# The seams between five parts of a layer stack, reordered by token tile, and the last expert step in half tiles

## The chip, the cores and the metric

The kernel runs on one core of a Trainium2 chip. TensorE (PE) multiplies, VectorE (DVE) and ScalarE (ACT) do elementwise work and read PSUM, GpSimd (POOL) does small things here (the powers of the norms, memsets, a few DMA issues), and SyncE (SP) issues most DMAs. Each engine works through its own instructions in order and waits on semaphores for the others. The metric is device time in microseconds of one launch.

## The reference, cut to what matters

Three blocks run one after the other on 256 tokens of width 1024, all in float32. The first ends in a 16-expert feed-forward layer and a norm. The second is two dense half layers around a token mixing (projections, a convolution, a chunked matrix memory, an output projection). The third is a stack of attention and recurrent layers, and its first step is a norm and a projection of the same 256 tokens.

```python
def rmsnorm(x, g):
    xf = x.astype(jnp.float32)
    y = xf * lax.rsqrt(jnp.mean(xf * xf, axis=-1, keepdims=True) + EPS)
    return (y * g.astype(jnp.float32)).astype(x.dtype)
...
    xl_new = xl_new + gt2 * expert_choice_ffn(modulate(xl_new, g_ffn, sh2, sc2), w_router, w1, w3, w2)
...
    return rmsnorm(xl, g_final)
...
def half_ffn(h, shift, scale, gate, g_pre, g_post, w13, w2):
    u = modulate_2(rmsnorm_2(h, g_pre), shift, scale)
    return h + 0.5 * gate * rmsnorm_2(swiglu(u, w13, w2), g_post)
...
        h_lat = half_ffn(h_lat, ml[:, 0], ml[:, 1], ml[:, 2], g[0], g[1], w13_a[l], w2_a[l])
        h_lat, h_ctx_new = token_mixing(
            h_lat, h_ctx, (ml[:, 3], ml[:, 4], ml[:, 5]), (mc[:, 3], mc[:, 4], mc[:, 5]),
            g[2], g[3], w_in[l], b_in[l], conv_w[l], conv_b[l], head_g[l],
            w_four[l], w_mproj[l], w_out[l], not last)
        h_lat = half_ffn(h_lat, ml[:, 6], ml[:, 7], ml[:, 8], g[4], g[5], w13_b[l], w2_b[l])
```

Each of these parts therefore ends in a sum over the whole width (a norm needs the mean square of a token's 1024 numbers), and the next part begins with one.

## The kernel before

The residual stream `x` lies in SBUF as two token tiles, t = 0 and 1, of 128 tokens by 1024. The weights stream from HBM in tiles of 128x2048 (1 MB) through a ring of buffers; `load` takes the next buffer and issues the DMA from SP.

Outside the experts a float32 product is made of three products in the faster `fp32r` form: each operand is split into a high and a low part, `wh` on ACT (L273) and `wl = w - wh` on DVE (L274) for weights, `uh` and `ul` (L364, L365) for activations, and `mm` (L282 to L284) multiplies three of the four pairs. Plain float32 products appear in the trace as two instructions each.

A part begins with `norm_T`: `norm_diag` takes the sum of squares of each token tile on ACT (L311), `rstd` makes the reciprocal root on POOL (L290, L291), a diagonal matrix `diag` is made of it on DVE (L314), and `to_T` multiplies x by that matrix on PE (L335, tile `pt`), which transposes and scales at once. ACT and DVE then take the result out of PSUM in turn (`val`, L356 and L360) with the part's scale and shift, and split it. Each PSUM tile of `to_T` holds both token tiles of two of the eight 128-wide slices of the width, so both tiles must be normed before the first slice is whole.

A part ends with `post`: for each token tile a square of the 128x1024 result (ACT, L961), `rstd`, a product with the gate `Gb` (DVE, L964) and the sum into x (DVE, L965).

- Experts: `experts` ends each group of four experts with products `py` (L912) over eight steps of four weight tiles. The last step sorts its products by weight tile, so that they follow the tiles as they land. The result is scattered by products `pcm` (L923) and added to x (L924). `final1` is the block's last norm, full width per token tile, and writes x.
- `ffn("a")` and `ffn("b")`: 22 steps f, each with 48 products `pu` of 128 weight columns by 256 tokens, a silu, and 12 products `py` (128x512) into two accumulators py0 and py1, one for each token tile. The products of step f's `py` stand behind step f+1's `pu`. After the last step comes `post`, and after that `ada2`, which makes one vector of the modulation (64 products `pa`, L399, a DMA of 4 MB).
- `mixing`: gate weights and gate products `pg` first, then k and q projections `pj`, then the value projection `proj_v` (96 products `pp` of 128x512), then the state stage. It ends with `po`, four weight tiles by two token tiles, `post` and `ada2`.
- `block3`: its first weight tile (j = 0) gives 48 products `pl` of 272 columns (16 extra tokens and the 256), in two accumulators.

The order within an engine follows the program, except that a scheduler moves instructions whose operands come late behind others, so the order of each engine has to be read from the built program.

Of the kernel before, what the change touches and what calls it, by code (L numbers as in the profile page):

```python
# [229 lines left out]
class Kern:  # L230
# [21 lines left out]

    def load(self, src, n=2048, dt=F32):

        p = self.slots.pop(0)
        self.slots.append(p)
        w = p.tile([128, 2048], F32, tag="w", name="w")
        self.nc.sync.dma_start(w[:, :n], src)
        return w[:, :n]
# [17 lines left out]
    def mm(self, out, l, r, start, stop):  # L277

        if len(l) == 1:
            self.nc.tensor.matmul(out, l[0], r[0], start=start, stop=stop)  # L280
        else:
            self.nc.tensor.matmul(out, l[0], r[0], start=start, stop=False)  # L282
            self.nc.tensor.matmul(out, l[0], r[1], start=False, stop=False)  # L283
            self.nc.tensor.matmul(out, l[1], r[0], start=False, stop=stop)  # L284

    def rstd(self, ss, n, w):
# [4 lines left out]
        nc.gpsimd.tensor_tensor(r[:, :w], v[:, :w], self.mhalf[:, :w], op=OP.pow)  # L291
# [12 lines left out]
    def norm_diag(self, h):  # L304

        nc = self.nc
        ds = []
        for t in range(2):
            sq = self.scr.tile([128, 1024], F32, tag="scr", name="sq")
            ss = self.sm.tile([128, 1], F32, tag="ss", name="ss")  # L310
            nc.scalar.activation(sq, h[:, t], AF.Square, accum_out=ss)  # L311
            r = self.rstd(ss, 1024, 1)
            d = self.sm.tile([128, 128], F32, tag="diag", name="diag", bufs=2)
            nc.vector.tensor_scalar(d, self.ident, r, None, op0=OP.mult)  # L314
            ds.append(d)
        return ds
# [563 lines left out]
    def experts(self, pool, gt2R, p1):  # L880
# [4 lines left out]
        self.bcast(gt2[:, :, 0], 8, gt2b)  # L885

        for g in range(4):
# [16 lines left out]
            for fp in range(8):  # L904
                b = (g * 8 + fp) * 4
                ts = [self.load(a["w2"][b + j]) for j in range(4)]
                order = [(i, n, j) for i in range(2) for n in range(2) for j in range(4)]
# [9 lines left out]
            for n in range(2):  # L917
                nc.vector.tensor_tensor(ye[:, n], py[:, n], gt2b[:, n * 512:(n + 1) * 512], op=OP.mult)
            for t in range(2):
                pc = self.psm.tile([128, 2, 512], F32, tag="m", name="pcm")  # L920
                for n in range(2):
                    sl = slice(n * 512, (n + 1) * 512)
                    nc.tensor.matmul(pc[:, n], self.Gt[:, g, t * 128:(t + 1) * 128], ye[:, n], start=True, stop=True)  # L923
# [285 lines left out]
    def ffn(self, s, A, B, gate, adas, after, pool):  # L1209
# [15 lines left out]
        for f in range(22):  # L1225
# [14 lines left out]
            if prev:  # L1240
                down(*prev)
# [703 lines left out]
```

## Time and profile before

| | |
|---|---|
| median of three runs | 2260.08 us (2259.12 to 2261.39) |
| profiled execution | 2256.84 us, its span 2255.0 us |
| busy, share of the span | PE 88%, weight load 60%, DVE 35%, ACT 27%, POOL 4% |
| mean granted clock of PE | 0.955 |

Until about 1273 us the 16 experts' weights stream in and the DMA engines are full. The dense parts behind them are bound by PE, and between two parts there is a gap of 12 to 20 us in which PE has little to do. In the answers by stage the columns behind the window and its length are busy us and instructions (x) of PE, weight load, DVE, ACT and POOL, then the granted share of PE's clock, the DMA engines' busy share and GB/s. A row of the timeline gives the start, the length, engine, line, the instruction with what it writes and reads, and in brackets how long the engine was idle before it and who released it.

### The profile page before, as it was taken

What the parts mean: (1) busy time and instruction counts of PE and PEld (TensorE: products, weight loads), DVE (VectorE), ACT (ScalarE), POOL (GpSimd) and SP (SyncE); (2) the same over time, 40 slices, a digit from 0 to 9 for tenths busy, and PEclk for the clock granted to TensorE, in tenths of its full rate; (3) what the DMA queues carried; (4) which work ended last, traced back from release to release, by engine and by line L of the source; (5) the groups of instructions that cost most, each with busy time, mean ns of one, the idle gap of its engine ahead of it and who ended that gap; (6) DMA issues with size and microseconds to landing.
All of it is one profiled execution on the core that took longest, in us unless ns stands there. A gap on an engine that the chain in (4) does not pass through costs nothing.

```text
span 2255.0 us, 29344 instructions
## 1 busy us (share of the span) xinstructions
PE 1990.1 (88%) x12348; PEld 1343.4 (60%) x12348; DVE 784.2 (35%) x1327; ACT 609.9 (27%) x1012; POOL 99.8 (4%) x182
## 2 busy tenths in 40 slices
PE   6998788888877888798887699989999999989997
PEld 4664334444434222243232399989889799978886
DVE  4464000000000000122011366557655555555666
ACT  4342100000000000011000244445444444445564
POOL 2200000000000000000000100010000000021030
PEclk9999899999999999999999999999999999999998
DMA  9669999999999999999999867534135655524221
GB/s 374 254 270 388 420 419 420 419 409 420 420 419 420 420 419 418 420 416 418 420 417 418 353 245 259 182 132 171 54 133 189 244 188 195 186 76 144 100 94 57
DMA packets 93268, 666.19 MB, mean 295 GB/s; under 512 B 10352, under 2 KB 10736, under 8 KB 13392
## 3 DMA queue, kind: packets, MB, share of 16 engines
q1 hardware_dynamic: 92416, 661.99, 74.1%
q8 instruction: 97, 1.59, 0.3%
q0 software_dynamic: 576, 2.10, 0.2%
q10 hardware_dynamic: 144, 0.23, 0.0%
q14 instruction: 35, 0.29, 0.0%
HBM read 663.23 MB, written 1.05 MB: 295 GB/s over the span
## 4 chain that ended last, share of the span: by engine, by line
PE 56%; DMA 25%; issue 10%; DVE 4%; ACT 3%; POOL 1%; SPq 0%; POOLq 0%; DVEq 0%; ACTq 0%
DMA w<-in_w_dram 23%; PE pu L874 7%; PE pu L1092 6%; PE py L912 4%; PE pd L1106 3%; PE pj L284 2%; PE pj L282 2%; PE pj L283 2%; PE pu L282 2%; PE pu L284 2%; PE pu L283 2%; DMA w<-in_w_mod_dram 2%; PE pl L282 1%; PE pl L284 1%; PE pl L283 1%
## 5 line engine op out<-in xcount | busy, mean ns | idle before, releaser
L874 PE MATMUL pu<-w,xe 128*32 128x512 f32 x2048 | 354.2, 668 | 97.4 <-DMA w<-in_w_dram 97.4
L274 DVE TENSOR_TENSOR wl<-w,wh 128x1024 fp32r<-128x1024 f32 (+1 forms) x286 | 348.2, 1221 | 236.2 <-ACT wh L273 236.0
L273 ACT ACTIVATE wh<-w 128x1024 fp32r<-128x1024 f32 (+1 forms) x286 | 299.5, 1053 | 329.0 <-PE pu L283 86.4
L874 PEld LDWEIGHTS pu<-w,xe 128*32 128x32 f32 x2048 | 80.9, 119 | 349.2 <-DMA w<-in_w_dram 187.9
L912 PE MATMUL py<-w,hT 128*32 128x512 f32 x1024 | 181.5, 641 | 65.6 <-DMA w<-in_w_dram 65.6
L283 PE MATMUL pu<-ul,wh 128*128 128x256 f32 x704 | 199.8, 284 | 1.1 <-DVE ul L365 1.1
L282 PE MATMUL pu<-uh,wh 128*128 128x256 f32 x704 | 200.1, 284 | 0.6 <-ACT uh L364 0.5
L284 PE MATMUL pu<-uh,wl 128*128 128x256 f32 x704 | 199.8, 284 | 0.8 <-DVE wl L274 0.8
L1092 PE MATMUL pu<-xu,w 128*128 128x256 f32 x704 | 157.8, 382 | 0.0
L912 PEld LDWEIGHTS py<-w,hT 128*32 128x32 f32 x1024 | 40.4, 115 | 195.5 <-DMA w<-in_w_dram 120.3
L1092 PEld LDWEIGHTS pu<-xu,w 128*128 128x128 f32 x704 | 131.9, 190 | 35.5 <-issue 18.4
L1097 DVE TENSOR_TENSOR xhT<-xs,pu 128x256 f32<-128x256 f32 x22 | 9.3, 421 | 381.6 <-ACT xs L1096 369.5
L283 PEld LDWEIGHTS pu<-ul,wh 128*128 128x128 f32 x704 | 135.6, 193 | 3.0 <-DVE ul L365 1.5
L282 PEld LDWEIGHTS pu<-uh,wh 128*128 128x128 f32 x704 | 135.5, 193 | 2.5 <-ACT uh L364 0.7
L284 PEld LDWEIGHTS pu<-uh,wl 128*128 128x128 f32 x704 | 135.5, 193 | 1.2 <-DVE wl L274 1.2
L1096 ACT ACTIVATE xs<-pu 128x256 f32<-128x256 f32 x22 | 8.4, 383 | 396.7 <-PE pu L1092 396.7
L284 PE MATMUL pj<-mu,wl 128*128 128x256 f32 x320 | 90.9, 285 | 4.4 <-DVE wl L274 4.4
L282 PE MATMUL pj<-mu,wh 128*128 128x256 f32 x320 | 91.0, 285 | 0.3 <-DVE val L1453 0.3
L283 PE MATMUL pj<-mu,wh 128*128 128x256 f32 x320 | 90.7, 283 | 0.0
L290 POOL TENSOR_SCALAR rs_v<-ss 128x1 f32<-128x1 f32 (+2 forms) x36 | 12.6, 351 | 1548.6 <-DVE ss L1116 690.1
L896 DVE TENSOR_TENSOR sil<-sil,pu 128x1024 f32<-128x1024 f32 x8 | 9.8, 1221 | 200.0 <-PE pu L874 200.0
L1106 PE MATMUL pd<-w,xhT 128*128 128x512 f32 x176 | 78.5, 599 | 0.0
(632 smaller groups left out, 3236.4 us busy)
## 6 DMA issues: line engine op xcount, KB each, us to landing
w<-in_w_dram SPq DMA_DIRECT2D x384, 1024.0 KB, 11.9
w<-in_w13a_dram SPq DMA_DIRECT2D x44, 1024.0 KB, 9.0
w<-in_w_ada_dram SPq DMA_DIRECT2D x36, 1024.0 KB, 7.3
w<-in_w_mod_dram SPq DMA_DIRECT2D x24, 1024.0 KB, 9.7
w<-in_w2a_dram SPq DMA_DIRECT2D x22, 1024.0 KB, 9.0
w<-in_w13b_dram SPq DMA_DIRECT2D x22, 1024.0 KB, 4.9
w<-in_w2b_dram SPq DMA_DIRECT2D x11, 1024.0 KB, 4.9
w<-in_w_out_dram SPq DMA_DIRECT2D x8, 1024.0 KB, 4.9
```

The source lines that it names most:

```text
L273: self.nc.scalar.activation(hi, v, AF.Copy)
L274: self.nc.vector.tensor_tensor(lo, v, hi.bitcast(F32), op=OP.subtract)
L282: self.nc.tensor.matmul(out, l[0], r[0], start=start, stop=False)
L283: self.nc.tensor.matmul(out, l[0], r[1], start=False, stop=False)
L284: self.nc.tensor.matmul(out, l[1], r[0], start=False, stop=stop)
L290: nc.gpsimd.tensor_scalar(v[:, :w], ss, 1.0 / n, EPS, op0=OP.mult, op1=OP.add)
L874: last = nc.tensor.matmul(ps[32 * j:32 * j + 32, n], self.xe[:, k, e * 32:(e + 1) * 32], ts[j][:, i * 1024 + n * 512:i * 1024 + (n + 1) * ...
L896: nc.vector.tensor_tensor(hid, s, p3.rearrange("p n c -> p (n c)"), op=OP.mult)
L912: last = nc.tensor.matmul(py[32 * j:32 * j + 32, n], hT[:, f, 32 * j:32 * j + 32], ts[j][:, i * 1024 + n * 512:i * 1024 + (n + 1) * 512], ...
L1092: nc.tensor.matmul(ps[:, ab * 256:(ab + 1) * 256], w[:, k * 256 + ab * 128:k * 256 + (ab + 1) * 128], uT[:, k], start=(k == 0), stop=(k == 7))
L1097: nc.vector.tensor_tensor(hT[:, f], s, ps[:, 256:], op=OP.mult)
L1106: nc.tensor.matmul(py[t][n], hT[:, f, t * 128:(t + 1) * 128], w[:, i * 1024 + n * 512:i * 1024 + (n + 1) * 512], start=(f == 0), stop=(f = ...
```

## The change

The last step of the experts loads each weight tile as two halves, first halves first, and its products follow in that order. The last norm of the experts works on halves of the width: y = x times the gain, squares of x and of y by halves, and the next part's norm is worked out from the two sums (`final1` returns y and the two diagonals). `norm_diag1`, `diag` and `to_T2` replace `norm_diag` and `to_T` here: a PSUM tile of `to_T2` holds four slices of one token tile. `post` works by halves (512 wide), where DVE takes one half while ACT squares the other, and ends with the next part's norm of that tile, so that it returns the diagonals. The dense halves hold back the `py` products of the last three steps and give them first to tile 0 and then to tile 1; `po` does the same with its last four slices. The first products of `mixing`, `ffn("b")` and `block3` are given by token tile: transposes of tile 0, its products, transposes of tile 1, its products. For `ffn("b")` and `block3` these products have 128 (or 144) columns instead of 256 (272). In `mixing` the first products are now those of `proj_v`. `ada2` of part 6 is moved from behind `ffn("a")` to ahead of its norm, and some memsets and DMAs of POOL behind the powers.

```diff
+    def to_T2(self, xn, A, B, outs, ds, off=0, ts=(0, 1)):
+        for t in ts:
+            for kh in range(2):
+                ps = self.psc.tile([128, 512], F32, tag="c", name="pt")
+                for i in range(4):
+                    k = 4 * kh + i
+                    nc.tensor.matmul(ps[:, i * 128:(i + 1) * 128], xn[:, t, k * 128:(k + 1) * 128], ds[t],
+                                     start=True, stop=True)
...
+                for i in range(4):
+                    k = 4 * kh + i
+                    vi, pi = v[:, i * 128:(i + 1) * 128], ps[:, i * 128:(i + 1) * 128]
+                    if i % 2 == 0:
+                        nc.scalar.activation(vi, pi, AF.Identity, scale=A[:, k], bias=0.0 if B is None else B[:, k])
...
+                        nc.vector.tensor_scalar(vi, pi, A[:, k], B[:, k], op0=OP.mult, op1=OP.add)
...
+                self.parts(v.rearrange("p (i n) -> p i n", i=4), [q[:, 4 * kh:4 * kh + 4, o:o + 128] for q in outs])
...
                 if g == 3 and fp == 7:
-                    order.sort(key=lambda v: v[2])
-                for i, n, j in order:
+                    ts = [self.slot() for j in range(4)]
+                    for i in range(2):
+                        for j in range(4):
+                            nc.sync.dma_start(ts[j][:, i * 1024:(i + 1) * 1024],
+                                              a["w2"][b + j][:, i * 1024:(i + 1) * 1024])
...
+        for n in range(2):
+            sl = slice(n * 512, (n + 1) * 512)
             for t in range(2):
...
+                nc.vector.tensor_tensor(y[:, t, sl], x[:, t, sl], gf[:, sl], op=OP.mult)
+                for w, src in ((0, x), (1, y)):
+                    sq = self.scr.tile([128, 1024], F32, tag="scr", name="sq")
+                    nc.scalar.activation(sq[:, :512], src[:, t, sl], AF.Square, accum_out=s8[:, w, t, n:n + 1])
...
     def post(self, h, py, Gb):
...
+            for n in range(2):
+                o, m = n * 512, (1 - n) * 512
+                nc.scalar.activation(sq[:, o:o + 512], py[t][:, n], AF.Square, accum_out=s2[:, n:n + 1])
+                nc.vector.tensor_tensor(tm[:, m:m + 512], py[t][:, 1 - n], Gb[:, m:m + 512], op=OP.mult)
             ss = self.sm.tile([128, 1], F32, tag="ss", name="ss")
-            nc.scalar.activation(sq, p, AF.Square, accum_out=ss)
+            nc.vector.tensor_tensor(ss, s2[:, 0:1], s2[:, 1:2], op=OP.add)
             r = self.rstd(ss, 1024, 1)
-            tm = self.scr.tile([128, 1024], F32, tag="scr", name="tmp")
-            nc.vector.tensor_tensor(tm, p, Gb, op=OP.mult)
             nc.vector.scalar_tensor_tensor(h[:, t], tm, r, h[:, t], op0=OP.mult, op1=OP.add)
+            ds.append(self.norm_diag1(h, t))
+        return ds
...
+            cols = [slice(0, 128), slice(128, 256)] if s == "b" and f == 0 else [slice(0, 256)]
+            last = None
+            for t, c in enumerate(cols):
+                if len(cols) > 1:
+                    with self.tc.issue_after(last.ins) if last else nullcontext():
+                        self.to_T2(src, A[:, :, 0:1], B[:, :, 0:1], uT, ds, ts=(t,))
+                for ab in range(2):
+                    for k in range(8):
+                        last = self.mm(ps[:, ab * 256 + c.start:ab * 256 + c.stop], w.at(k * 256 + ab * 128, 128),
+                                [q[:, k, c] for q in uT], k == 0, k == 7)
...
+        for t in range(2):
+            for v in left:
+                down(*v, (t,))
+        return self.post(x, py, Gb)
...
+        ws = [self.wload(a["w_out2"][kp]) for kp in range(4)]
+
+        for k, t in [(k, t) for k in range(4) for t in range(2)] + [(k, t) for t in range(2) for k in range(4, 8)]:
```

`issue_after` lets what stands under it be ordered only behind the named instruction. The order on the engines that comes out is shown at three places.

The first place is ACT between mixing and dense half b. `po_` with a number is the accumulator of a token tile, `sq` a square, `wh` the high part of a weight tile of half b, `val` the transposed rows out of PSUM and `uh` their high part. Before:

```order
L961 ACTIVATE sq,ss<-po_10360 128x1024
L961 ACTIVATE sq,ss<-po_10361 128x1024
L311 ACTIVATE sq,ss<-x 128x1024 x2
L273 ACTIVATE wh<-w 128x1024 x2
L356 ACTIVATE val<-pt,m_6_7670,A_4_10577 128x256
L273 ACTIVATE wh<-w 128x1024
L364 ACTIVATE uh<-val 128x256
```

and with the change:

```order
L1015 ACTIVATE sq,s_10508<-po_10370 128x512 x2
L314 ACTIVATE sq,ss<-x 128x1024
L1015 ACTIVATE sq,s_10531<-po_10371 128x512 x2
L314 ACTIVATE sq,ss<-x 128x1024
L276 ACTIVATE wh<-w 128x1024 x2
L337 ACTIVATE val<-pt,m_6_5707,A_4_10613 128x128 x2
L276 ACTIVATE wh<-w 128x1024 x2
L337 ACTIVATE val<-pt,m_6_5707,A_4_10613 128x128 x2
L391 ACTIVATE uh<-val 128x4x128 x2
L276 ACTIVATE wh<-w 128x1024
L337 ACTIVATE val<-pt,m_6_5707,A_4_10613 128x128 x4
L391 ACTIVATE uh<-val 128x4x128 x2
```

The squares of tile 1's result and of its x still stand ahead of the first `val` of tile 0, and four weight halves instead of two or three stand ahead of the first `uh`.

The second place is PE at the same seam, where `pa` is the modulation, `pt` the transposes and `pu` the first products of half b. Before:

```order
L284 MATMUL po_10361<-wh,yTl 128x512
L399 MATMUL pa<-w,s_112 32x256 x32
L410 MATMUL pat<-ident,adaR 128x128 x2
L335 MATMUL pt<-diag,x 128x128 x16
L282 MATMUL pu<-uh,wh 128x256
```

and with the change:

```order
L287 MATMUL po_10371<-wh,yTl 128x512
L426 MATMUL pa<-w,s_112 32x256 x32
L437 MATMUL pat<-ident,adaR 128x128 x2
L330 MATMUL pt<-diag,x 128x128 x8
L285 MATMUL pu<-uh,wh 128x128
L286 MATMUL pu<-ul,wh 128x128
```

The transposes of both tiles no longer stand together: eight of tile 0 are followed by 48 products of 128 columns, and behind the last of these come the eight of tile 1 with 48 more.

The third place is DVE between the experts and dense half a, where `yf` is x times the gain, `sums` are small sums, `wl` low parts of weights and `val`, `ul` the rows for the first products. With the change:

```order
L319 TENSOR_SCALAR diag<-ident,sums 128x128 x2
L439 TENSOR_TENSOR m_6_5707<-pat,cols 128x16
L341 TENSOR_SCALAR val<-pt,A_0_2124,m_0_1148 128x128
L277 TENSOR_TENSOR wl<-w,wh 128x1024
L341 TENSOR_SCALAR val<-pt,A_0_2124,m_0_1148 128x128 x2
L277 TENSOR_TENSOR wl<-w,wh 128x1024
L392 TENSOR_TENSOR ul<-val,uh 128x4x128
L341 TENSOR_SCALAR val<-pt,A_0_2124,m_0_1148 128x128
L277 TENSOR_TENSOR wl<-w,wh 128x1024
L392 TENSOR_TENSOR ul<-val,uh 128x4x128
```

Before, all five `wl` of this stretch stood ahead of the first `val`, among the additions and the norms; now they stand between the `val` rows.

## Rows read from the trace of the kernel before

**Rows 1.** Busy time by stage: the four gaps between last and first products; column heads above

```profile
core 0: us, PE busy (x) PEld busy (x) DVE busy (x) ACT busy (x) POOL busy (x), PEclk, DMA share, GB/s
1273.60:1293.10 19.50, 10.65 (x41) 7.77 (x41) 15.11 (x22) 11.28 (x20) 5.70 (x8) 0.74 0.77 300
1485.60:1500.40 14.80, 10.52 (x100) 8.39 (x99) 10.01 (x22) 8.78 (x16) 7.34 (x17) 0.78 0.52 196
1776.80:1788.60 11.80, 9.46 (x100) 7.36 (x99) 9.59 (x14) 7.83 (x14) 4.79 (x8) 0.86 0.84 333
1788.60:1797.20 8.60, 6.59 (x35) 5.55 (x35) 7.04 (x13) 5.13 (x11) 0.00 (x0) 0.83 0.80 299
1983.40:1997.20 13.80, 5.54 (x34) 5.54 (x33) 9.55 (x12) 5.58 (x13) 7.46 (x11) 0.63 0.00 0
```

**Rows 2.** Groups of instructions, shapes apart, whole span: busy us, mean ns of one

```profile
L274 DVE TENSOR_TENSOR wl<-w,wh 128x1024 fp32r<-128x1024 f32 x283 | 346.1, 1226 | 236.2 <-ACT wh L273 236.0
...
L273 ACT ACTIVATE wh<-w 128x1024 fp32r<-128x1024 f32 x283 | 297.6, 1058 | 327.5 <-PE pu L283 86.4 <-DMA w<-in_w13a_dram 76.8 <-issue 49.7
...
L924 DVE TENSOR_TENSOR x<-x,pcm 128x512 f32<-128x512 f32 x16 | 11.0, 687 | 4.5 <-PE pcm L923 4.5
...
L965 DVE SCALAR_TENSOR_TENSOR x<-tmp,rs_r,x 128x1024 f32<-128x1024 f32 x6 | 7.7, 1288 | 0.6
...
L243 ACT ACTIVATE hT<-pht 128x512 f32<-128x512 f32 x8 | 4.8, 597 | 167.0 <-DVE hT L245 122.5 <-PE pht L899 44.6
...
L356 ACT ACTIVATE val<-pt,m,A 128x256 f32<-128x256 f32 x12 | 6.7, 555 | 4.8 <-PE pt L335 4.7
...
L291 POOL TENSOR_TENSOR rs_r<-rs_v,mhalf 128x1 f32<-128x1 f32 x32 | 21.5, 673 | 2.4
```

**Rows 3.** Timeline around the end of the experts: start us, us, engine, line, instruction

```profile
1267.45 6.12 PE L912 MATMUL py<-w,hT 128*32 128x512 f32 x18
...
1273.61 1.29 DVE L918 TENSOR_TENSOR ye<-py,gt2b 128x512 f32<-128x512 f32 x2 [71.20 <-PE py L912]
...
1286.19 1.62 PE L335 MATMUL pt<-diag,x 128*128 128x128 f32 x6 [7.95 <-DVE diag L314]
...
1293.07 0.36 PE L282 MATMUL pu<-uh,wh 128*128 128x256 f32 x1
```

**Rows 4.** Timeline, dense half a into mixing

```profile
1484.39 1.03 ACT L961 ACTIVATE sq<-py 128x1024 f32<-128x1024 f32 x1 [1.69 <-PE py L284]
...
1488.19 1.06 ACT L311 ACTIVATE sq<-x 128x1024 f32<-128x1024 f32 x1 [1.26 <-DVE x L965]
...
1500.30 0.56 PE L282 MATMUL pg<-mu,wh 128*128 128x256 f32 x1
```

**Rows 5.** Timeline, mixing into dense half b, all engines, and TensorE a little later

```profile
1776.82 3.66 PE L399 MATMUL pa<-w,s 128*32 128x256 f32 x64
...
1788.56 0.36 PE L282 MATMUL pu<-uh,wh 128*128 128x256 f32 x1
...
1796.12 0.41 PE L282 MATMUL pu<-uh,wh 128*128 128x256 f32 x1
...
1796.34 0.41 PE L283 MATMUL pu<-ul,wh 128*128 128x256 f32 x1
```

**Rows 6.** Timeline, dense half b into block3

```profile
1983.02 0.39 PE L284 MATMUL py<-wh,fhl 128*128 128x512 f32 x1
...
1991.67 5.76 PE L335 MATMUL pt<-diag,x 128*128 128x128 f32 x32 [8.26 <-DVE diag L314]
...
1997.18 0.37 PE L282 MATMUL pl<-xTh,wh 128*128 128x272 f32 x1
```

**Rows 7.** Timeline, TensorE inside dense half a

```profile
1299.98 0.28 PE L282 MATMUL pu<-uh,wh 128*128 128x256 f32 x1
...
1300.10 0.28 PE L283 MATMUL pu<-ul,wh 128*128 128x256 f32 x1
...
1332.95 1.84 PE L435 MATMUL pa<-ones,aacc 128*128 128x1 f32 x16
```

More of the change, by code (lines that the diff above doesn't have):

```diff
@@ L1 @@
 import math
[L2 removed]
+from contextlib import ExitStack, contextmanager, nullcontext
 import numpy as np
@@ L279, in mm @@
         if len(l) == 1:
-            self.nc.tensor.matmul(out, l[0], r[0], start=start, stop=stop)
+            return self.nc.tensor.matmul(out, l[0], r[0], start=start, stop=stop)
         else:
@@ L917, in experts @@
             for n in range(2):
-                nc.vector.tensor_tensor(ye[:, n], py[:, n], gt2b[:, n * 512:(n + 1) * 512], op=OP.mult)
-            for t in range(2):
[L920 to L923, printed above, removed]
-                    nc.vector.tensor_tensor(x[:, t, sl], x[:, t, sl], pc[:, n], op=OP.add)
@@ L1036, in proj_T, with by_token @@
         return ps
-    def by_token(self, srcs, uT, split=True):
+    def by_token(self, srcs, uT, split=True, by_t=None):
         ps = [self.psc.tile([128, 512], F32, tag="c", name="pp") for t in range(2)]
+        if by_t:
+            ws = [self.wload(w, split=split) for w in srcs]
+            last = None
+            for t in range(2):
+                by_t(t, last)
+                for k in range(8):
+                    last = self.mm(ps[t], [q[:, k, t * 128:(t + 1) * 128] for q in uT], ws[k // 4].at((k % 4) * 512, 512),
+                            k == 0, k == 7)
+            return ps
         for h in range(2):
@@ L1047, in by_token, with proj_v @@
         return ps
-    def proj_v(self, w_ap, uT, split, bvb, vaug):
+    def proj_v(self, w_ap, uT, split, bvb, vaug, by_t=None):
         nc = self.nc
         for n in range(2):
-            pv = self.by_token([w_ap[2 * n + i] for i in range(2)], uT, split)
+            pv = self.by_token([w_ap[2 * n + i] for i in range(2)], uT, split, None if n else by_t)
             for t in range(2):
@@ L1286, in mixing @@
         nc.vector.memset(nMA, 0.0)
-        nc.gpsimd.memset(rows[:, 2], 0.0)
+        with self.tc.issue_after(behind.ins):
+            nc.gpsimd.memset(rows[:, 2], 0.0)
         for p0, ca, cb, d in ((0, 0, 1, 0), (32, 1, 0, 1)):
@@ L1567, in lin, with lin_by_t @@
             return ps[:, :T - o]
+        def lin_by_t(wt, uT):
+            ps = [self.psc.tile([128, 512], F32, tag="c", name="pl") for _ in range(2)]
+            last = None
+            for t, (c0, c1) in enumerate(((0, 144), (144, 272))):
+                with self.tc.issue_after(last.ins) if last else nullcontext():
+                    self.to_T2(x, self.col("a_norm").unsqueeze(2), None, uT, ds, 16, (t,))
+                for i in range(2):
+                    for k in range(8):
+                        last = self.mm(ps[i][:, c0:c1], wt.at(k * 256 + i * 128, 128), [q[:, k, c0:c1] for q in uT],
+                                k == 0, k == 7)
+            return [p[:, :T] for p in ps]
         aes = ExitStack()
```

178 lines of the change are left out of this document (104 added, 74 removed).

## The prediction

> **What bounds the kernel now.** I read the answer by stage first. The experts are bound by the DMA engines and the dense parts by PE, so what this change can win lies in the four gaps between parts, and those I read window by window [rows 1]. The reader is to see a gap's length, how little PE does in it and that its clock falls: 19.5 us behind the experts (granted clock 0.74 of full), 14.8 us into mixing (0.78), 11.8 us into dense half b and 8.6 more in which PE runs only 35 products (0.83), 13.8 us into block3 (0.63). The clock has two levels, 1.2 and 2.4 GHz, and these means lie between them. Together some 68 us.
>
> What fills a gap is a chain, read from the timelines. Behind the experts: `ye` starts at 1273.61, the first transposes at 1286.19, the first product at 1293.07 [rows 3]. Into mixing the square of tile 0 starts at 1484.39, x of that tile is whole when its own square starts at 1488.19, 3.9 us after the tile's last product (about 1484.3), and the first product comes at 1500.30 [rows 4]. The other two gaps run from 1776.82 to 1788.56 [rows 5] and from 1983.4 to 1997.18, with the transposes of both tiles (32 instructions in 5.76) at their end [rows 6].
>
> The change wants tile 0 to go through this chain while PE still multiplies for tile 1, and tile 1's chain to lie under tile 0's first products. Whether it can depends on two things: how long PE is busy in each case, and whether ACT and DVE, which work in order, take tile 0 first.
>
> **How much cover there is.** In the dense halves only 13 products of tile 1 stand behind the last one of tile 0. A 128x512 product takes about 0.23 us (that is the spacing of the `py` rows ahead of 1983.02 [rows 6]; estimate from twice the 0.12 of a 256-column one [rows 7]), so they give 3.0 us. `po` gives 24 of them, 5.5 us. The chain of tile 0, from its last product to its first transposed rows, is longer than either, as follows.
>
> **Prices.** A half operation on DVE 0.69, on ACT 0.60 [rows 2], plus an estimated 0.2 where ACT reads out a sum; the sum into x 1.29, `wh` 1.06, `wl` 1.23, a power 0.67 [rows 2] and about 0.9 with the scaling ahead of it; handing over 0.05 to 0.1 (x whole at 1488.15, its square at 1488.19 [rows 4]). `val` of 128x256 is 0.56 on ACT [rows 2]; of 128x128 I take 0.35 to 0.4, estimated (at the least half, 0.28).
>
> **`post` by halves.** In the built order each half waits for the other engine: ACT squares half 0, DVE multiplies half 1, ACT squares half 1, DVE multiplies half 0. Both read one PSUM tile, and each row waits for the row before. That is 0.8 + 0.75 + 0.8 + 0.75 + 0.2 = 3.3 us before the power, then 0.9 and 1.3: x at 5.5 us after the last product, against 3.9 before [rows 4]. So each tile's chain grows by 1.6 us.
>
> **Mixing into half b**, in us after tile 0's last product (tile 1's is at 5.5). x of tile 0 at 5.5; ACT squares it to 6.8; then, in ACT's order, come the two halves of tile 1, with DVE's in between and the first diagonal (7.9), to 10.3, the power to 11.3, x of tile 1 at 12.6. `pa` (3.66 [rows 5]) runs 5.5 to 9.2, but the copy of its result on DVE stands behind x of tile 1, so PE can begin tile 0's transposes only at 13.5. ACT meanwhile squares x of tile 1 (13.9) and splits two weight halves (16.0); only then `val` (16.4, and 17.2 for the second PSUM tile); two more `wh` (19.3); `val` twice more with DVE's `val` and a `wl` between; `uh` 21.0. The first product starts at 21, which is 15.5 after tile 1's last. Its second needs `ul`, which stands behind another `wl`: 17.0. Before it was 11.8 and then another 4.4 lost (8.6 us for 35 products of 0.12 [rows 1, 7]), 16.2 together. So the start itself costs about +0.8.
>
> Then there are two new costs. **A gap in the middle:** tile 1's transposes are ordered behind tile 0's last product. Four of them (eight instructions of about 0.11) take 0.9, four `val` in turn 1.9, `uh` 0.7, `ul` 0.7; minus the products that can start on `uh` alone it is 4.0 us of PE's time. **Narrow products:** 48 products of 256 columns become 96 of 128. No product of fp32r with fewer than 256 columns is in this trace. Below, 0.06 each, half the spacing of 256 columns (0.12 [rows 7]): nothing lost. Above, 0.21, the spacing that rows with 256 columns show at the lower clock [rows 5]: +14.4. The nearest row is that of `pa<-ones`, whose weights are as large and whose moving side is one column: 16 instructions in 1.84, 0.11 each, so here the weight load sets the pace [rows 7]. I take it: 96 x 0.11 - 48 x 0.12 = +4.8. Sum for this seam: 0.8 + 4.0 + 4.8 = +9.6.
>
> The Trainium skill's page "TensorE: Matmul & The Clock Gate" bears on the last price. Its section "LDWEIGHTS" gives columns / 1.2 in ns, 107 ns for 128 columns, which the row of 0.11 agrees with. Its section "Back-to-back issue gap" gives about 81 ns for each of a stream of weight load and product with 128 columns; by that, an estimate from the page, the narrow products would cost 2.0 us a seam and not 4.8. No run here shows 81 ns.
>
> **Half b into block3.** The same order: tile 1's last product at 3.0, POOL's memsets stand between the powers as before, and the same sum of steps gives the first product 14.9 us after tile 1's last one, against 13.8 [rows 1]. The middle gap of 4.0 and the narrow products (144 and 128 columns, +4.7) come on top: +9.8.
>
> **Half a into mixing.** By the same steps the first product comes 16.4 us after tile 1's last (before 14.8 [rows 1], with some 1.5 of stalls behind it). The middle gap adds 4.0. In the gap stands now the broadcast of the value bias (1.9 us of PE that before lay later), and the products stay wide, 128x512. 16.4 + 4.0 - 1.9 - 16.3 = +2.2.
>
> **Experts into half a.** Eight products followed the landing of the last whole tile; of a half tile it is four. At 0.34 each (18 in 6.12 [rows 3]) that is -1.4. The rest of the chain: additions and products with the gain interleaved on DVE, eight half squares on ACT to 9.4 us, three small sums and two powers, the diagonals at 13.3 (before, the first transposes began 12.6 after `ye` [rows 3]). So the norm itself is about level. But the rows for the first products then come through ACT and DVE one after the other with five `wh` and five `wl` between them, where before these splits lay in the wait for the norm. Counted through, first products 24 to 28 us after the experts' end, against 19.5 [rows 3]. With the -1.4 I take +4, bounds -2 and +6. `ada2` of part 6 goes ahead of the first weights of half a: 4 MB, at the 300 GB/s of that gap [rows 1] 14 us, so these weights land as much later, about when ACT comes to them; that is hidden just so. Its 3.7 us of products [rows 5] leave the next seam, where they lay beside the chain and cost nothing.
>
> **Inside mixing** `proj_v` no longer stands between the last convolution and the state stage, and up to 2 us of that chain comes out: +1.
>
> **Sum.** 4 + 2.2 + 1 + 9.6 + 9.8 = +26.6 us on the profiled execution's 2256.84 (its span of 2255.0 and 1.8 around it), 2283.4. The median of the runs shown is 3.2 higher than that execution. I say 2285.
>
> **The rivals.**
> *Narrow products at the price of the lower clock*, 0.21 each. For it: PE stands almost still for 15 us ahead of them, and behind such waits the trace has 256 columns at 0.21 [rows 5]. Against: that lasted a few us only. Both seams then cost 9.6 more each: about 2304.
> *Cheap narrow products and short chains*: 0.06 to 0.08 each, and the steps of ACT and DVE overlap better than I have them, by 2 us a seam: 2285 - 8 - 8 = 2269.
> *The first tile does get ahead* (faster). In three seams tile 0's rows would be split before tile 1's are needed, the middle gap is covered, and PE never stands long enough for its clock to fall. This saves what the gaps now lose: the first product about 7 us after tile 1's last in place of 12 to 15, three times, -21 with the clock, and -1.4 at the experts, with +9.5 for narrow products: about 2247 to 2250. It decides at the `val` of tile 0: if it starts before the squares of tile 1, the change wins. Against it stands ACT's order, in which it is behind them.
> *It comes out level*: the shorter waits pay exactly for the narrow products, about 2260.
>
> **Chances.** Forecast 0.60 (its own range 2272 to 2296), dear narrow products 0.13, cheap ones 0.10, faster 0.11, level 0.06. A difference of 0.2%, 4.5 us, is about what a measurement of this kernel tells from no change. So faster 0.11, same 0.07, slower 0.82. The range that leaves out some 2 in 10 goes from 2257 to 2305.
>
> **What would show it.** In the changed profile: `val` of tile 0 on ACT behind both squares of tile 1 in three seams; first products 15 to 17 us after the last ones; a second gap of about 4 us between two groups of 48 products at half b and block3, with 128-column products at 0.11. The prediction is wrong if the narrow ones run at 0.06 or 0.21, if the middle gap is missing, or if the gap behind the experts shrinks.

## The result, and the profile after

The changed kernel takes 2312.45 us (median of four runs, 2311.17 to 2314.35), the kernel before in the same comparison 2260.6. The ratio is 1.0231 with a 95% interval of 1.0213 to 1.0249: slower by 52 us, about twice the 26.6 that the sum gave. The profiled execution took 2314.35 us with a span of 2312.6; PE's mean granted clock fell from 0.955 to 0.937.

Where the 57.6 us between the two profiled spans lie is read from the starts of rows that both traces have, which cut the program into stretches (us):

| stretch | before | after | difference | in the sum |
|---|---|---|---|---|
| to `ye` of the last expert half | 1274.2 | 1273.5 | -0.7 | (in the next) |
| to the first `pa<-ones` of half a: experts' seam | 58.7 | 68.7 | +10.0 | +4 |
| to the first state product `psT`: half a and the seam into mixing | 252.9 | 258.5 | +5.6 | +3.2 |
| to the last silu of half b: mixing and the seam into half b | 390.4 | 412.4 | +22.0 | +9.6 |
| to the first sum of `kvl` in block3: the seam into block3 | 46.6 | 66.7 | +20.1 | +9.8 |
| from there to the last `sq` of `hT` | 120.5 | 121.7 | +1.2 | 0 |
| to the end | 111.7 | 111.1 | -0.6 | 0 |

The stretch that ends with `hT` is the same code in all kernels and varies from 120.5 to 125.0 among the runs below, so a microsecond or two there is no effect of an edit, and the kernel before was profiled at the short end of it. The last silu is not quite the same mark in both kernels: it starts 7.2 us ahead of the end of half b's last product before, and 6.0 with the change (1976.2 to 1983.4, 2013.1 to 2019.1). So 1.2 us of the +22.0 belong to the next stretch.

The changed kernel by stage, with the columns of [rows 1]: two windows at the experts' seam, one into mixing, eight around half b, four around block3.

```profile
1272.80:1298.90 26.10, 14.56 (x108) 9.15 (x107) 17.40 (x33) 14.69 (x33) 2.23 (x4) 0.80 0.93 377
1298.90:1305.40 6.50, 5.91 (x26) 5.61 (x27) 2.35 (x4) 0.92 (x2) 0.00 (x0) 0.50 0.45 161
1491.00:1511.60 20.60, 10.09 (x52) 8.76 (x51) 13.33 (x28) 11.39 (x23) 6.49 (x14) 0.72 0.34 113
1791.80:1805.80 14.00, 5.86 (x83) 3.99 (x82) 8.94 (x17) 9.14 (x18) 2.23 (x6) 0.93 0.84 331
1804.00:1805.80 1.80, 0.00 (x0) 0.00 (x0) 1.80 (x4) 1.35 (x4) 0.00 (x0) 0.50 0.80 291
1805.80:1817.30 11.50, 10.56 (x48) 10.37 (x49) 3.10 (x4) 1.44 (x2) 0.00 (x0) 0.50 0.41 153
1817.30:1823.00 5.70, 3.72 (x17) 3.43 (x17) 1.58 (x4) 2.26 (x6) 0.00 (x0) 0.68 0.00 0
1823.00:1824.30 1.30, 1.04 (x7) 0.84 (x7) 1.29 (x2) 0.57 (x1) 0.00 (x0) 1.00 0.00 0
1824.30:1833.30 9.00, 9.00 (x45) 9.00 (x44) 1.23 (x2) 1.06 (x1) 0.00 (x0) 0.50 0.00 0
1833.30:1838.10 4.80, 4.80 (x25) 4.80 (x25) 2.07 (x3) 3.14 (x4) 0.00 (x0) 0.51 0.60 218
1838.10:1848.00 9.90, 9.90 (x74) 9.41 (x73) 4.43 (x5) 3.75 (x5) 0.00 (x0) 1.00 0.37 117
2019.10:2033.30 14.20, 3.80 (x17) 3.54 (x17) 6.11 (x14) 5.63 (x15) 6.24 (x11) 0.61 0.00 0
2033.30:2043.90 10.60, 10.58 (x49) 10.38 (x49) 1.23 (x2) 0.42 (x1) 0.00 (x0) 0.50 0.01 2
2043.90:2049.50 5.60, 4.31 (x26) 3.91 (x25) 2.00 (x5) 2.36 (x6) 0.00 (x0) 0.79 0.00 0
2049.50:2058.20 8.70, 8.70 (x44) 8.70 (x43) 1.92 (x2) 2.20 (x5) 0.00 (x0) 0.51 0.00 0
```

The reader is to compare PE's busy time with the clock beside it. At half b PE has little to do for 14.0 us, and at the end of that time its granted clock is at 0.50, the lower of the two levels. There it stays while the 48 narrow products of tile 0 run. Behind the transposes of the middle gap (5.7 us) tile 1's group begins at 1.00, but 1.3 us later the clock falls again, with PE busy, and the other products run at 0.50 to their end. Some 24 products of 256 columns follow at 0.51, and then the clock is at 1.00 up to the next seam. Block3 reads alike: 14.2 us of waiting, 10.6 us at 0.50, a window of 5.6 (the middle gap of 4.3 and the first products behind it) in which the clock rises among the transposes, 8.7 us at 0.51.

The timeline of the changed kernel at these places, with the columns of [rows 3]:

```profile
1286.76 0.48 DVE L319 TENSOR_SCALAR diag<-ident,sums 128x128 f32<-128x128 f32 x2
...
1298.90 0.79 PE L285 MATMUL pu<-uh,wh 128*128 128x256 f32 x2 [5.70 <-ACT uh L391]
...
1511.60 0.80 PE L285 MATMUL pp<-wh,mu 128*128 128x512 f32 x1 [6.38 <-ACT mu L391]
...
1523.76 0.63 PE L285 MATMUL pp<-wh,mu 128*128 128x512 f32 x1 [2.01 <-ACT mu L391]
...
1785.85 0.40 PE L287 MATMUL po<-wh,yTl 128*128 128x512 f32 x1
...
1786.28 0.60 ACT L1015 ACTIVATE sq<-po 128x512 f32<-128x512 f32 x1 [4.54 <-PE po L287]
...
1787.00 0.69 DVE L1016 TENSOR_TENSOR tmp<-po,Gb 128x512 f32<-128x512 f32 x1 [4.01 <-ACT sq L1015]
...
1787.73 0.60 ACT L1015 ACTIVATE sq<-po 128x512 f32<-128x512 f32 x1 [0.76 <-DVE tmp L1016]
...
1788.45 0.69 DVE L1016 TENSOR_TENSOR tmp<-po,Gb 128x512 f32<-128x512 f32 x1 [0.76 <-ACT sq L1015]
...
1790.16 1.28 DVE L1020 SCALAR_TENSOR_TENSOR x<-tmp,rs_r,x 128x1024 f32<-128x1024 f32 x1 [0.95 <-POOL rs_r L294]
...
1798.37 1.06 ACT L314 ACTIVATE sq<-x 128x1024 f32<-128x1024 f32 x1 [3.11 <-DVE x L1020]
...
1801.32 0.79 ACT L337 ACTIVATE val<-pt,m,A 128x128 f32<-128x128 f32 x2
...
1805.83 0.48 PE L285 MATMUL pu<-uh,wh 128*128 128x128 f32 x1 [4.94 <-ACT uh L391]
...
1807.22 0.47 PE L286 MATMUL pu<-ul,wh 128*128 128x128 f32 x1 [0.91 <-DVE ul L392]
...
1809.62 0.41 PE L285 MATMUL pu<-uh,wh 128*128 128x128 f32 x1
...
1809.84 0.41 PE L286 MATMUL pu<-ul,wh 128*128 128x128 f32 x1
...
1823.03 0.50 PE L285 MATMUL pu<-uh,wh 128*128 128x128 f32 x2 [2.01 <-ACT uh L391]
...
1837.71 0.41 PE L285 MATMUL pu<-uh,wh 128*128 128x256 f32 x1
...
1837.92 0.32 PE L286 MATMUL pu<-ul,wh 128*128 128x256 f32 x1
...
1838.08 0.28 PE L287 MATMUL pu<-uh,wl 128*128 128x256 f32 x1
...
2033.25 0.70 PE L285 MATMUL pl<-xTh,wh 128*128 128x144 f32 x2 [5.32 <-ACT xTh L391]
...
2043.87 3.12 PE L330 MATMUL pt<-diag,x 128*128 128x128 f32 x16
...
2048.16 0.61 PE L285 MATMUL pl<-xTh,wh 128*128 128x128 f32 x3 [1.18 <-ACT xTh L391]
...
2058.12 0.54 PE L286 MATMUL pl<-xTl,wh 128*128 128x272 f32 x1
```

Two starts that follow each other give the price: 1809.62 and 1809.84, about 0.21 for a product of 128 columns (48 of them in the 10.1 us from 1807.2 to 1817.3: 0.21). The three rows from 1837.71 on show the clock rise among products of 256 columns: their own time falls from 0.41 to 0.28. The last four rows bound block3's two groups and the middle gap between them. The four rows of `sq` and `tmp` show `post` by halves in turn, 0.72 from start to start, each released by the row before.

### The profile page after: what moved, and what is told of

Read it like the earlier page. It is cut to its first block, busy times and chain, and to the rows that moved or that the text cites. A ratio compares the mean times of both kernels' runs of the same rounds, so it can differ in the third digit from the quotient of the medians.

```text
span 2312.6 us, 29562 instructions
## 1 busy us (share of the span) xinstructions
PE 2031.6 (88%) x12444; PEld 1379.2 (60%) x12444; DVE 787.3 (34%) x1347; ACT 614.0 (27%) x1032; POOL 94.3 (4%) x178
## 4 chain that ended last, share of the span: by engine, by line
PE 63%; DMA 26%; DVE 5%; ACT 3%; POOL 2%; issue 1%; SPq 0%; DVEq 0%; POOLq 0%; ACTq 0%
DMA w<-in_w_dram 24%; PE pu L1158 6%; PE pu L901 6%; PE pu L286 4%; PE pu L287 4%; PE pu L285 4%; PE py L945 3%; PE pd L1172 3%; PE pj L287 2%; PE pj L285 2%; PE pj L286 2%; PE pl L286 2%; PE pl L285 2%; PE pl L287 2%; PE py L285 2%; PE py L286 2%
## 5 line engine op out<-in xcount | busy, mean ns | idle before, releaser
L285 PE MATMUL pu<-uh,wh 128*128 128x256 f32 (+1 forms) x720 | 210.3, 293 | 12.6 <-ACT uh L391 12.6
L286 PE MATMUL pu<-ul,wh 128*128 128x256 f32 (+1 forms) x720 | 210.0, 292 | 1.7 <-DVE ul L392 1.7
L287 PE MATMUL pu<-uh,wl 128*128 128x256 f32 (+1 forms) x720 | 210.1, 292 | 0.0
L285 PEld LDWEIGHTS pu<-uh,wh 128*128 128x128 f32 x720 | 144.3, 201 | 15.7 <-ACT uh L391 13.3
L286 PEld LDWEIGHTS pu<-ul,wh 128*128 128x128 f32 x720 | 144.4, 201 | 3.7 <-DVE ul L392 2.4
L287 PEld LDWEIGHTS pu<-uh,wl 128*128 128x128 f32 x720 | 144.3, 200 | 1.0 <-DVE wl L277 1.0
L426 PE MATMUL pa<-w,s 128*32 128x256 f32 x832 | 56.8, 415 | 16.6 <-ACT s L411 8.4
```

The costliest lines, as they stand in the source:

```text
L287: return self.nc.tensor.matmul(out, l[1], r[0], start=False, stop=stop)
L426: nc.tensor.matmul(ps[32 * j:32 * j + 32, :256], s[:, k, :], t[:, i * 1024 + j * 256:i * 1024 + (j + 1) * 256], start=(k == 0), stop=(k == ...
```

## The experiments

Each run is compared with the kernel before on the same chip, so the median of before differs a little between groups of runs. Stretches are those of the table above. The ratio is that of the record, with a 95% interval, and not exactly the quotient of the two medians.

### The narrow products: undone, and alone

In the first kernel the last two seams take both tiles together again: rows of both tiles first, then 48 products of full width. All else is the change. This removes the middle gap with the narrow products.

```diff
-        if s == "a":
-            self.to_T2(src, A[:, :, 0:1], B[:, :, 0:1], uT, ds)
+        self.to_T2(src, A[:, :, 0:1], B[:, :, 0:1], uT, ds)
...
-            cols = [slice(0, 128), slice(128, 256)] if s == "b" and f == 0 else [slice(0, 256)]
+            cols = [slice(0, 256)]
...
```

> The changed kernel, with the first products of dense half b and of block3 undivided again (both tiles' transposes, then 48 products of 256 or 272 columns); all else as changed. Theory A (the 128-column products run at 0.21 us each because the clock stays at 1.2 GHz while they do, and the second tile's transposes open a second gap of 5 us): both seams give back 12 to 16 us each, the time is 2281 to 2288, 24 to 31 under the changed kernel. Rival B (what costs is the chain ahead of the first product, and the narrow products cost little): less than 10 us comes back, over 2302.

Measured: 2280.99 us against 2257.09, ratio 1.0093 (1.0073 to 1.0113). The seam into half b gives back 16.0 us (412.4 to 396.4) and the one into block3 16.0 (66.7 to 50.7). Of the change's +22.0 and +20.1 there remain +6.0 and +4.1. So three quarters of the loss in these two seams come from taking the first products by tile.

The second kernel is the counterpart: the kernel before, with nothing but its first products of half b and of block3 split into 128 columns (144 and 128 in block3). It has no middle gap.

```diff
+            cols = [slice(0,128), slice(128,256)] if s == "b" and f == 0 else [slice(0,256)]
+            for c in cols:
...
-                            [q[:, k] for q in uT], k == 0, k == 7)
+                                [q[:, k, c] for q in uT], k == 0, k == 7)
...
```

> The kernel before, with one thing of the change: the first products of dense half b and of block3 are 96 of 128 (or 144) columns in two groups in place of 48 of 256 (272); transposes and rows as before, so that into block3 they start with the clock at 2.4 GHz. Theory A1 (a stream of 128-column products lets the clock fall, and each then takes 0.21): about +15 us a seam with the slow wide products behind it, 2288 to 2295, and 0.50 granted during them although the engine is busy all the time. Theory A2 (they were slow only because the clock had fallen in the wait ahead of them): about +5 us at block3 at 0.11 each, and 5 to 10 at half b, 2270 to 2276. Theory C (they cost 0.06): level with before.

Measured: 2280.62 us against 2257.09, ratio 1.0102 (1.0075 to 1.0128). The seam into half b is 12.4 us longer than before, that into block3 5.8: there as expected for 0.11 each, at half b more than the 5 to 10 expected. Four windows of this kernel, with the columns of [rows 1]: half b's products from their start, the narrow ones behind them (80, with 5 of 256 columns among them), the first ones of 256 columns after that, and block3's 95 narrow products with the four that follow:

```profile
1788.40:1794.30 5.90, 3.61 (x23) 2.87 (x22) 5.88 (x11) 4.72 (x10) 0.00 (x0) 1.00 0.90 321
1794.60:1812.40 17.80, 17.80 (x85) 17.80 (x85) 2.09 (x3) 1.69 (x3) 0.00 (x0) 0.50 0.06 26
1812.40:1814.60 2.20, 2.20 (x11) 2.20 (x11) 1.23 (x1) 2.17 (x3) 0.00 (x0) 0.50 0.63 190
...
2010.40:2021.80 11.40, 11.12 (x99) 10.97 (x99) 3.08 (x8) 4.14 (x10) 0.00 (x0) 1.00 0.01 1
```

These are the rows on which the case turns: the same kind of product, PE busy nearly from end to end, and a factor of nearly two. 85 in 17.8 us (0.21 each) at the lower level, 99 in 11.4 us (0.11 to 0.12) at the upper one. The price on record, 0.11, is that of the upper level. At half b the products begin at 1.00, but stop and start (2.3 us of the 5.9 without work); at 1794.3 the clock falls, and in 17.8 us of work without a pause it does not rise. In block3 they run on almost without a stop and the clock stays.

### The clock itself: products that nobody needs

If the clock that fell in the wait is what makes the narrow products dear, then keeping PE at work in the wait must make them cheap. `fill` puts products of the identity with a constant tile, 456 columns wide, into the waits; their result is not used. In the changed kernel, six at the end of half b, six and two behind the two transposes at half b, six and three at block3:

```diff
...
+    def fill(self, n, after):
+        ps = self.psc.tile([128, 512], F32, tag="c", name="pz")
+        with self.tc.issue_after(after.ins):
+            for i in range(n):
+                last = self.nc.tensor.matmul(ps[:, :456], self.ident, self.cols[:, :456], start=True, stop=True)
+        return last
...
-                        self.to_T2(src, A[:, :, 0:1], B[:, :, 0:1], uT, ds, ts=(t,))
+                        pe = self.to_T2(src, A[:, :, 0:1], B[:, :, 0:1], uT, ds, ts=(t,))
+                    self.fill((6, 2)[t], pe)
...
```

> The changed kernel with products of no use (`ident` by 456 columns of a constant, into a PSUM tile that nobody reads) added on TensorE where it waits at the seams of half b and block3: six behind half b's last product, six behind the transposes of tile 0, two or three behind those of tile 1. Theory K (the 128-column products take 0.11 at 2.4 GHz and 0.21 only because the clock fell in the wait ahead of them and does not rise while they run): with the clock held through the waits they take 0.11, and 20 to 32 us come back although work was added; ratio 1.009 to 1.014. Rival D (the chain ahead of them decides; when the engine is faster it waits longer): less than 8 us come back, ratio over 1.019.

Measured: 2297.1 us against 2260.7, ratio 1.0157 (1.0142 to 1.0172). Its four groups of narrow products by stage, tile 0 and tile 1 of half b, then of block3; the second and the third are cut where the clock falls:

```profile
1803.80:1809.20 5.40, 5.37 (x48) 5.37 (x49) 1.72 (x2) 0.03 (x1) 0.00 (x0) 1.00 0.60 206
1813.90:1815.90 2.00, 2.00 (x18) 2.00 (x19) 0.52 (x1) 0.00 (x0) 0.00 (x0) 1.00 0.00 0
1815.90:1822.00 6.10, 6.10 (x31) 6.10 (x31) 1.23 (x1) 1.06 (x1) 0.00 (x0) 0.51 0.00 0
2022.50:2024.20 1.70, 1.70 (x15) 1.70 (x16) 0.53 (x1) 0.00 (x0) 0.00 (x0) 1.00 0.00 0
2024.20:2030.80 6.60, 6.60 (x33) 6.60 (x33) 0.00 (x0) 0.00 (x0) 0.00 (x0) 0.50 0.00 0
2036.50:2042.20 5.70, 5.70 (x51) 5.51 (x49) 0.90 (x2) 2.52 (x4) 0.00 (x0) 1.00 0.01 3
```

All four groups begin at 1.00 now. Two keep it, at 0.11 a product; in the other two the clock falls 2 us after the start, while PE is busy, and the rest costs 0.20 each. The timeline of the same kernel shows what stands ahead of one of each kind, the third and the fourth:

```profile
2021.76 0.44 PE L285 MATMUL pl<-xTh,wh 128*128 128x144 f32 x2 [2.53 <-ACT xTh L399]
2022.48 0.33 PE L286 MATMUL pl<-xTl,wh 128*128 128x144 f32 x1 [0.28 <-DVE xTl L400]
...
2036.49 0.58 PE L285 MATMUL pl<-xTh,wh 128*128 128x128 f32 x1
```

The one that falls had a wait of 2.53 us behind the last filling product, the one that stays had none. The seams gave back 7.7 and 6.6 us and the span 15.5. That the clock sets the price is shown (products that compute nothing make the kernel faster, and each narrow one costs what the level of its stretch says); the size was about half of what was hoped for, as the filling held the clock for two groups only.

The same filling in the kernel before, 9 products behind the experts, 5 into mixing, 2 into half b and 9 into block3, with nothing of the change:

> The kernel before with products of no use on TensorE in its four waits (nine behind the last additions' products of the experts, five and two behind the modulations, nine behind half b's last product). If the clock that falls in these waits costs something of its own, the transposes behind them take 0.11 to 0.12 an instruction in place of 0.18 to 0.21, and 5 to 10 us are saved, ratio 0.9955 to 0.998. If the chain on ACT, DVE and POOL sets the end of each wait anyway, 0 to -2 us, ratio over 0.999.

Measured: 2253.26 us against 2260.7, ratio 0.9960 (0.9946 to 0.9974), faster than both kernels: all its five runs (2249.35 to 2255.74) lie below the sixteen of before (2256.54 to 2263.20). Two of its windows by stage, at the experts' seam and into mixing, where before had 0.74 and 0.78 [rows 1]:

```profile
1274.90:1294.00 19.10, 17.30 (x77) 10.79 (x78) 15.61 (x24) 11.78 (x23) 5.70 (x8) 1.00 0.78 310
1484.00:1500.00 16.00, 14.64 (x124) 10.07 (x122) 9.34 (x20) 8.29 (x15) 7.35 (x17) 1.00 0.47 181
```

And the group of transposes, shapes apart, with the columns of [rows 2], first in the kernel before and then in this one:

```profile
L335 PE MATMUL pt<-diag,x 128*128 128x128 f32 x128 | 24.9, 376 | 20.7 <-DVE diag L314 20.6
...
L342 PE MATMUL pt<-diag,x 128*128 128x128 f32 x128 | 16.2, 280 | 4.3 <-DVE diag L314 4.3
```

The clock is 1.00 through both gaps and a transpose takes 280 ns in place of 376. The stretches of the four seams are 1.5, 0, 2.5 and 0.9 us shorter; `ye` is 0.7 later and the `hT` stretch 3.1 longer, so the two profiled spans differ by 1.0 us only, and the gain rests on the medians.

### The experts' seam: norm, evictions, ada2

Three kernels undo one thing each in the changed kernel. One takes back the old norm of the last block and the old `norm_T` in half a, and with them the transposes with both tiles in each PSUM tile:

```diff
...
-            self.to_T2(src, A[:, :, 0:1], B[:, :, 0:1], uT, ds)
+            self.norm_T(x, A[:, :, 0:1], B[:, :, 0:1], uT)
```

> The changed kernel, with the experts' last norm and dense half a's norm as before (full width, per tile) and the old transposes and evictions there; the modulation vector stays ahead of half a and the last expert step in half tiles. Theory N (the norm by halves and the eviction by four slices cost the 10 us of this seam): 8 to 10 us come back, 2303 to 2305. Theory S (the modulation's 4 MB ahead of half a's weights push the splits of these weights between the rows of the first products, whichever norm it is): less than 4 us come back.

Measured: 2306.08 us against 2257.09, ratio 1.0208 (1.0189 to 1.0227). The seam goes from 68.7 to 59.1, against 58.7 before: 9.6 of the 10.0 are given back. A narrower kernel keeps the new norm and takes back the old transposes alone:

```diff
-            self.to_T2(src, A[:, :, 0:1], B[:, :, 0:1], uT, ds)
+            self.to_T(src, A[:, :, 0:1], B[:, :, 0:1], uT, 0, ds)
```

> The changed kernel with the old transposes and evictions (two slices of both tiles in a PSUM tile) ahead of dense half a alone; the norm by halves and the modulation ahead of half a stay. It splits the 8 us that the old norm and the old rows together gave back in this seam. If the four serial rows of a PSUM tile, and the first slice that is whole only when all four PSUM tiles' halves of it are out, cost it: 4 to 7 us come back in the stretch from the scatter to the first reduction in half a (68.7 in the changed kernel, 59.1 with old norm and old rows). If the norm by halves does: 0 to 2 us.

Measured: 2307.28 us against 2258.16, ratio 1.0215 (1.0201 to 1.0229). The seam is 62.2, so the rows by tile cost 6.5 of the 10.0, and 3.1 are left for the norm by halves. Some 2 of the 6.5 are the clock's: with the old rows the first products (from 1294.80) start 0.12 apart, in the changed kernel some 24 of them 0.21 apart. The third moves `ada2` of half a back behind `post`:

```diff
-        self.ada2(first)
...
-        return self.post(x, py, Gb)
+        ds = self.post(x, py, Gb)
+        self.ada2(first)
+        return ds
```

> The changed kernel, with the modulation vector of part 6 behind dense half a again; the norm by halves stays. Theory S: the weights' splits lie in the wait for the norm again, the first product of half a comes 5 to 6 us earlier and the seam gives back 5 to 9 us; the seam into mixing loses 0 to 3 by it; 2304 to 2309. Theory N: nothing comes back, 2312 to 2315.

Measured: 2308.64 us against 2257.09, ratio 1.0219 (1.0197 to 1.0241), the seam 65.3: 3.4 back, less than the 5 to 9 expected. With `ada2`'s 4 MB ahead, the first weight tile of half a is asked for at 1272.42 in place of 1264.55, and the splits meet the evictions on ACT and DVE: in the changed kernel ACT's first `wh` (1289.63) stands behind the first `val` (1289.28), for which ACT had waited 6.2 us, and the others between the `val` rows; with `ada2` moved back all five stand ahead of the first `val`. The three gains together (9.6 for norm and rows, 3.4) exceed the loss, so they overlap; how they divide is read from single profiled executions and holds to about a microsecond.

### Parts of the change alone in the kernel before

`post` by halves, without its norm:

```diff
...
+            for n in range(2):
+                o, m = n * 512, (1 - n) * 512
+                nc.scalar.activation(sq[:, o:o + 512], py[t][:, n], AF.Square, accum_out=s2[:, n:n + 1])
+                nc.vector.tensor_tensor(tm[:, m:m + 512], py[t][:, 1 - n], Gb[:, m:m + 512], op=OP.mult)
...
```

> The kernel before with `post` by halves of 512, all else as before. If the halves run one behind the other between ACT and DVE, as the order says, x of a tile comes 1.6 us later and, as both tiles go through, each of three seams loses 1.6 to 3.2: +5 to +9 us, ratio 1.002 to 1.004. If the two engines overlap as the code's order of halves suggests, 0 to -3 us, ratio 0.9985 to 1.000.

Measured: 2267.42 us against 2260.7, ratio 1.0023 (1.0011 to 1.0035): slower, by 1.0 us in the seam into half b and 4.9 in the one into block3, with nothing (0.1) in the one into mixing. The last expert step in half tiles:

```diff
...
+                    for i in range(2):
+                        for j in range(4):
+                            nc.sync.dma_start(ts[j][:, i * 1024:(i + 1) * 1024],
+                                              a["w2"][b + j][:, i * 1024:(i + 1) * 1024])
...
```

> The kernel before with the last expert step in half tiles, all else as before: the experts end 0.7 to 1.4 us earlier, and so does the kernel, ratio 0.9994 to 0.9997, too little to be told in time; the trace shows it by the start of ye against the last landing.

Measured: 2256.99 us against 2260.7, ratio 0.9990 (0.9980 to 0.9999), with `ye` 1.2 us earlier: a gain below what can be told from no change. The products of the last steps held back, so that all of tile 0's stand ahead of tile 1's, in `po` too:

```diff
...
+        for t in range(2):
+            for v in left:
+                down(*v, (t,))
...
```

> The kernel before with one thing of the change: the last three steps' products of the dense halves, and the last four slices of the mixing's output, first for tile 0 and then for tile 1. `post`, norms and first products as before. Tile 0's chain then ends before tile 1's begins, and only tile 1's stands in the gap: -1 to -2 us in each of three seams, -3 to -5 together, ratio 0.998 to 0.9987. If the chains don't overlap on ACT and DVE, or the held-back products cost more elsewhere: 0 to +2.

Measured: 2257.45 us against 2258.16, ratio 0.9992 (0.9983 to 1.0001), not told from no change; its seams into half b and block3 are 2.1 and 1.6 shorter, which the varying `hT` stretch (124.8) covers.

### Versions put together

The kernel before with the filling and the half tiles:

> The kernel before with the added products of no use in its four waits and with the last expert step in half tiles. The two have nothing to do with each other, so their savings add: ratio 0.9945 to 0.996.

Measured: 2253.0 us (nine runs) against 2258.16, ratio 0.9973 (0.9964 to 0.9983), the half tiles adding nothing that could be told beside the filling alone (0.9960, 0.9946 to 0.9974). With the held-back products as well:

> The same with the held-back products as well. If holding back is worth 3 to 5 us alone it is worth them here, ratio 0.992 to 0.9945; the added products were sized for the waits as they were, so up to 1 us a seam may be lost where the wait is now shorter than they are.

Measured: 2256.25 us against 2258.16, ratio 0.9986 (0.9978 to 0.9995): no better. The filled kernels before, with half tiles or without, are the fastest that were run.

## Why the prediction was right or wrong

**The sign, and what was right.** The decisive step held: `val` of tile 0 (1801.32) stands behind the squares of tile 1 on ACT (the last at 1798.37), so the first tile doesn't get ahead. Tile 1's last product of `po` ends at 1791.8, and the first narrow product comes 14.0 us later, a running stream at 1807.2, 15.4 later (on record 15.5 and 17.0). Into mixing it is 16.1 from the last `py` (1495.5) to 1511.60 (on record 16.4), with a middle gap of 3.8 (on record 4.0). Into block3 the wait is 14.2 (14.9). `post` by halves gives x of tile 0 at 1791.44, 5.2 us after the tile's last product (5.5), and alone it makes the kernel slower. The chains were counted rightly.

**The step that failed** is the price of the narrow products: "The nearest row is that of `pa<-ones` … 0.11 each, so here the weight load sets the pace … I take it". That row was at the upper level of the clock, and so is every narrow product at 1.00 above (0.11 to 0.12). But the products stand behind waits (14.0 us, then 2.0 in the middle gap), the clock has fallen in the one and falls soon after the other, and it does not come back while they run. The rival "Narrow products at the price of the lower clock", with 0.13, is what came, and 0.21 was one of the signs named for being wrong. Its 2304 is still 8 us short; the largest part of that is the experts' seam, 6.0 over its term. The argument against it, "that lasted a few us only", was read from products of 256 columns [rows 5] and does not carry over to 128.

The seam into half b can be added up with what was measured: the two groups last 10.1 and 10.3 us in place of 48 products at 0.12, 5.8, which is +14.6 (on record +4.8); the middle gap 5.7 (4.0), part of it transposes at the lower clock; the running start 15.4 in place of 16.2, -0.8 (+0.8); the 25 products behind, 0.19 each in place of 0.12, +1.8 (none on record). That is 21.3. Read straight from the rows, half b's first `py` starts 49.3 us behind mixing's last product (1841.08) in place of 29.1 (1805.96), +20.1, so the sum is about 1 us too high; most of the rest of the 22.0 is the 1.2 of the silu. For block3: groups of 10.6 and 10.0 and a middle gap of 4.3 in place of 48 products at the 0.127 of 272 columns, 6.1; +0.4 at the start; some 22 products of 272 columns behind them, still at the lower level, +2.2 (none on record); -1.2 for the silu. That is 20.2 of the 20.1.

**The experts' seam** is a mis-sized term: +4 was taken from bounds of -2 and +6, and it was +10.0. The prediction's own count, 24 to 28 in place of 19.5 and -1.4, makes +3.1 to +7.1, so +4 was its low end, and nothing in the count gives -2. First products were put at 24 to 28 us behind the end of the experts, and came at 26.1 (1298.90), with the stream at 1300.29. What the term lacked is what follows: some 24 products at the lower level up to 1305.4. "The norm itself is about level" was wrong by about 3 us, and the rows by tile cost 6.5. The weights of half a were to be "hidden just so" behind `ada2`; they were not, and putting `ada2` back gained 3.4.

**Into mixing and inside it** +3.2 was on record and +5.6 came, but four other kernels with the same code there (first products undone, filled, old transposes, old norm) have +2.2, +2.0, +1.8 and +4.2, so the term holds within what this stretch varies.

**The Trainium skill.** The page "TensorE: Matmul & The Clock Gate", section "LDWEIGHTS", gives columns / 1.2 in ns, by which 128 columns take 107 ns; the 0.11 of the products at 1.00 agrees with that and the 0.21 at 0.50 does not. Its section "Back-to-back issue gap" gives about 81 ns, which no run here showed for these products.

**What stays open.** Whether an order in which ACT and DVE really take tile 0 first would win was not tried. How the experts' 10 us divide exactly between rows, norm and `ada2`, is not settled. Why the clock falls soon after the start of some groups and not of others is not shown. It fell behind waits of 2.0, 1.2 and 2.5 us (1823.03 and 2048.16 in the changed kernel, 2021.76 in the filled one) and stayed in the fourth group of the filled kernel, which had none; but at tile 1 of half b in that kernel it fell behind two waits of 0.5 and 0.2 us (1813.14 and 1813.87), and the first group, with one of 0.4 ahead (1803.84), kept it.

## What to carry to other kernels

A price read from a row holds at that row's clock level: before summing up new small products, look at the granted clock of the stretch in which they will stand, and take the lower level's price if they begin behind a long wait. Splitting a part's first products by tile is meant to let the first tile come through ACT and DVE ahead of the second; here it did not (no run has an order in which it does), so read the order of these engines before counting on it. Where a wait can't be shortened, a few idle products in it may be worth more than a new order: here they made the kernel before 0.3 to 0.4% faster, and the whole change made it 2.3% slower.

## What the runs showed of the hardware

Not expected: a stretch in which PE was busy throughout stayed at the lower level of its clock. In the kernel before with narrow products alone, 85 products, 80 of them of 128 columns, ran for 17.8 us at 0.50 without a pause, while 95 narrow ones that began at 1.00 in block3, with almost no stop, stayed at 1.00. Behind the 17.8 us, and in the changed kernel from 1833.3 to 1838.1, products of 256 columns began at the lower level, and the clock rose to 1.00 among them, at 1814.7 and at 1838.0 (there behind some 24 of them). Whether it is their width that makes the difference no run here tells.
